# A mixer stage whose decay exponentials take their bias on ScalarE, whose GpSimd products and weight parts move to VectorE, and whose pooled and gate pieces take turns

## The chip, the cores and the metric

One core of a Trainium2 chip runs the whole program in a single launch. The metric is the device time of one execution in microseconds (us). The engines are named as in the profile: PE is TensorE (PEld its weight loads), DVE is VectorE, ACT is ScalarE, POOL is GpSimd, SP is SyncE, whose queue issues most of the loads.

## What is computed

Two transformer blocks in float32 for one sequence of 512 tokens and width 1024. The change touches only the first stage, the hybrid mixer of the first block:

```
proj = u @ w_in
z, xbc, dt_raw, v = split(proj)                        # gate, conv input, step size, pooled path
xbc = silu(causal_depthwise_conv(xbc, conv_w, conv_b))
xs, bm, cm = split(xbc)                                # 16 heads of 64; 2 groups of B and C
dt = softplus(dt_raw + dt_bias);  adt = dt * -exp(a_log)
a_cs = cumsum(adt)  in chunks of 128
seg = exp(where(causal, a_cs[l] - a_cs[s], -inf))      # decay, per head and chunk
y_diag = (C B^T * seg) @ (xs * dt)                     # within a chunk
y_off  = C @ carried_state * exp(a_cs)                 # from the chunks before
y = rmsnorm((y_diag + y_off + d_skip * xs) * silu(z))
y_pool = (window means of v, minus v) @ pool_w * pool_scale
h = x + concat(y, y_pool) @ w_out_mix
```

Cross attention, two gated MLPs, a stick-breaking attention and a sparse attention follow, and are the same before and after.

## The kernel before

Activations lie with features on the 128 partitions and the 512 tokens along the row. Float32 products of full accuracy are made of three matmuls: every operand is split into a high part in a reduced format and the low rest. A weight **piece** is 128 output features by 1024 inputs (1024 columns of float32, 512 KB); `Weights` fetches pieces on SP's queue in the order of the list that `_plan` writes, ScalarE makes the high part `wh` (L340), and `lo` makes the low part `wl` as a subtraction (L349): on VectorE, or on GpSimd for the seven pieces named in `POOL_LO` (L29): xs3, xs5, C1, v1, v4, v6 and v7. A piece is then 24 matmuls of 512 columns in `group` (all recorded at the helper's line L538). Parts are made up to two pieces ahead.

The order of all work is that of the Python text (the scheduler is manual); each engine takes its own instructions in that order. The mixer's function `_mix` (L709) runs:

- lead: B0, C0 and dt, while the input is split; then xs0.
- nine pieces xs1, xs2, xs3, B1, C1, xs4 to xs7 (L749). After each, `conv` (L880) runs a convolution on its result in three steps over three pieces: scaling and the first tap (L900, L903), three taps on VectorE (L906) and a tanh on ScalarE, and the final product (L914).
- in the background, one step after each piece: `g_dt` (L943), the step size. It ends in `adt` (L987), from which eight small matmuls form cumulated sums, and the matrix `stk` of split sums (L1006). A chain of a log series runs there, two operations per coefficient on GpSimd (L974 to L978), in a step of its own.
- `g_pair` (L1011), once for each of the eight xs pieces (two heads each), in three steps, none before `g_dt` has ended: step one transposes xs, makes `xc` and `xd` (L1025), spreads the cumulated sums over a bank by matmuls from `stk`, subtracts the column of sums `acs` on VectorE (L1035) and takes the exponential on ScalarE (L1038); step two makes the chunk states from `xd`, multiplies the decay `d` by the scores `cb` on GpSimd (L1052), and carries the states on (L1059); step three multiplies `d` by `xc` and the states by C on TensorE, and adds up (L1072 to L1074, the last on GpSimd).
- eight pooled pieces v0 to v7 (L758), each with 1 to 4 window additions on VectorE (`pool_v`, L1076), and behind every second of them the products with `pool_w` (`pool_mm`); then eight gate pieces z0 to z7 (L770), each with a tanh and two products (`g_z`, L785: L789 on VectorE, L791 on GpSimd, L793 on VectorE) and the sum of squares.

Banks of PSUM are taken from a pool of eight and go back when their readers are done.

Of the kernel before, what the change touches and what calls it, by code (L numbers as in the profile page):

```python
# [14 lines left out]
ALU = mybir.AluOpType  # L15
# [3 lines left out]
P = 128  # L19
# [9 lines left out]
POOL_LO = {"xs3", "xs5", "C1", "v1", "v4", "v6", "v7"}  # L29
# [3 lines left out]
NP = 8  # L33
FF_BLOCKS = ((0, 8), (8, 16), (16, 22))
# [13 lines left out]
def _plan(x, phases):  # L48
# [25 lines left out]
    if "mix" in phases:  # L74
# [14 lines left out]
        for j in range(8):  # L89
            add(f"v{j}", _bform(w, v0 + P * j, v0 + P * j + P))  # L90
            if j in (2, 4, 6):
                pw((j - 2) // 2)
        for j in range(8):
            add(f"z{j}", _bform(w, P * j, P * j + P))
            if j == 0:
                pw(3)
# [369 lines left out]
class Kernel:  # L466
# [242 lines left out]
    def _mix(self):  # L709
# [48 lines left out]
        for j in range(8):  # L758
            ps = self.bank()
            self.group(ps, self.W.get(f"v{j}"), xh, xl, range(KT), True, True)  # L760
            self.W.ahead()
            if j < 2:
                self.conv()
            dd[j] = self.pool_v(j, ps)
            self.W.lo()
            self.stage()
            if j in (2, 4, 6):
                self.pool_mm((j - 2) // 2, dd, self.yp)
        n2 = self.n2 = Norm(self, EPS_A, "ssd")
        for j in range(8):  # L770
            ps = self.bank()
            self.group(ps, self.W.get(f"z{j}"), xh, xl, range(KT), True, True)
            while any(p[2] <= j for p in self.pairs):
                self.stage(2)
            self.W.ahead()
            g = self.g_z(j, ps)
            next(g)
            self.W.lo()
            self.stage(3)
            self.bg.append(g)  # L780
            if j == 0:
                self.pool_mm(3, dd, self.yp)
        self.drain()

    def g_z(self, j, ps):  # L785

        nc, y = self.nc, self.y[:, j, :]
        t, th = self.tmp("t", bufs=3), self.tmp("pv", (P, 528), bufs=3)[:, :T]
        nc.vector.scalar_tensor_tensor(t, ps, 0.5, self.R, op0=ALU.mult, op1=ALU.mult)  # L789
        nc.scalar.activation(th, t, AF.Tanh)  # L790
        nc.gpsimd.tensor_tensor(t, t, y, op=ALU.mult)  # L791
        yield
        nc.vector.scalar_tensor_tensor(y, th, 1.0, t, op0=ALU.add, op1=ALU.mult)  # L793
        self.n2.tile(y)
# [128 lines left out]
    def g_cb(self, g):  # L923
# [14 lines left out]
        nc.vector.tensor_copy(cb, ps)  # L938
        nc.vector.tensor_copy(bt, pt[:, :384])
# [3 lines left out]
    def g_dt(self, ps, rtm):  # L943
# [29 lines left out]
        gp = nc.gpsimd  # L973
        gp.tensor_tensor(z2, z, z, op=ALU.mult)  # L974
        gp.tensor_scalar(q, z2, 1.0 / 17, 0.0, op0=ALU.mult, op1=ALU.add)
        for n in (15, 13, 11, 9, 7, 5, 3):
            gp.tensor_scalar(q, q, 1.0, 1.0 / n, op0=ALU.mult, op1=ALU.add)
            gp.tensor_tensor(q, q, z2, op=ALU.mult)  # L978
        yield
# [17 lines left out]
        acs, last = t64("acs"), t64("last")  # L997
        nc.vector.tensor_copy(acs, pa[:, 0:64].rearrange("p (c h) -> p c h", c=4))
        dec = t64("dec")
        tt(last, pa[:, 64:128].rearrange("p (c h) -> p c h", c=4), acs, ALU.subtract)  # L1000
# [8 lines left out]
        self.dt, self.acs, self.dec, self.cd = dt, acs, dec, cd  # L1009

    def g_pair(self, k):  # L1011
# [17 lines left out]
        for j in range(2):  # L1029
# [21 lines left out]
        for j in range(2):  # L1051
            nc.gpsimd.tensor_tensor(dm[j], dm[j], self.cbT[g], op=ALU.mult)  # L1052
# [1164 lines left out]
```

## Time and profile before

| | |
|---|---|
| runs of the kernel | 2213.94, 2212.48, 2205.34 us (median 2212.48) |
| the profiled execution | 2205.24 us, span 2203.5 us, mean granted clock 0.993 |
| PE busy | 2130.0 us, 97% of the span |
| PEld, DVE, ACT, POOL busy | 1730.3, 1231.0, 876.1, 261.2 us |
| the mixer stage | about the first 250 us of the span |

Matmuls are pipelined, so PE's busy time is not PE at its peak. A row of the windows view gives a stretch, its length, the busy time of each engine with the number of its instructions, PEclk (the share of full clock that was granted: 1.00 is 2.4 GHz, 0.50 is 1.2 GHz), the share of the DMA engines and GB/s. A row of the waits view names who waited for whom, the sum in us, how often, and the longest. A row of the groups view gives line, engine, operation, output and inputs, sizes and count, then the busy time in us and the mean of one in ns, then the idle time before them and what ended it. A row of the timeline gives start, duration, engine, line, operation and count; operations of an engine overlap a little at their ends, so the distance from one start to the next is what an operation costs in a queue.

### The profile page before, as it was taken

To read this page: it belongs to the slowest core of one execution; us is meant where nothing else is said; L and a number is where in the kernel's file an instruction comes from. 1 tells how busy PE (TensorE), PEld (TensorE's weight loads), DVE (VectorE), ACT (ScalarE), POOL (GpSimd) and SP (SyncE) were. 2 spreads that over 40 slices of the span, in tenths; PEclk is the share of its full clock that TensorE was granted. 3 is DMA by queue.
4 is the path that set the end of the run, shared out by engine and by line. 5 is a ranking of instruction groups with operands and counts; after the bars stand their busy time and mean duration, and the time that the engine had idled before them with its cause. 6 is when DMAs were issued, how large, how long until landed. Compare 5 with 4: busy or idle time off the path is not lost.

```text
span 2203.5 us, 26617 instructions
## 1 busy us (share of the span) xinstructions
PE 2130.0 (97%) x10250; PEld 1730.3 (79%) x10250; DVE 1231.0 (56%) x2032; ACT 876.1 (40%) x1405; POOL 261.2 (12%) x324
## 2 busy tenths in 40 slices
PE   8899999999999999999999999999988899999998
PEld 6687888888888888777688888888766668888886
DVE  6988756554443435567655343446668755534334
ACT  4424434343222224355534232334547644423322
POOL 1333100000000000122200000001037730000000
PEclk9999999999999999999999999999999999999999
DMA  4222444123333323322143333334431123333331
GB/s 147 63 72 77 134 122 152 57 72 96 97 97 101 98 84 108 124 77 67 48 124 97 104 95 97 96 96 127 129 98 26 26 60 103 109 101 97 96 97 66
DMA packets 63375, 205.93 MB, mean 93 GB/s; under 512 B 7952, under 2 KB 8336, under 8 KB 63120
## 3 DMA queue, kind: packets, MB, share of 16 engines
q1 hardware_dynamic: 59504, 196.86, 30.1%
q10 hardware_dynamic: 3744, 7.37, 1.0%
q8 instruction: 80, 1.31, 0.2%
q14 instruction: 47, 0.39, 0.1%
HBM read 189.39 MB, written 6.29 MB: 89 GB/s over the span
## 4 chain that ended last, share of the span: by engine, by line
PE 78%; DVE 10%; ACT 4%; POOL 4%; issue 3%; DMA 1%; SPq 0%; ACTq 0%; POOLq 0%; DVEq 0%
PE psum L538 62%; PE b L538 14%; POOL sph L1683 1%; DVE wl L349 1%; ACT sT L1665 1%; ACT sT L1666 1%; DVE t L906 1%; PE psum L2090 1%; DVE spl L1688 1%; DVE sT L1660 1%; DVE np L2068 1%; DMA nq<-nq 1%; DVE pv L1087 0%; DVE sT L1659 0%; POOL np L2082 0%
## 5 line engine op out<-in xcount | busy, mean ns | idle before, releaser
L538 PE MATMUL psum<-xh,wh 128*128 128x512 f32 x1560 | 609.9, 391 | 1.5 <-DVE h L626 0.9
L538 PE MATMUL psum<-xh,wl 128*128 128x512 f32 x1560 | 607.5, 389 | 1.6 <-DVE wl L349 1.5
L538 PE MATMUL psum<-xl,wh 128*128 128x512 f32 x1560 | 607.2, 389 | 0.0
L340 ACT ACTIVATE wh<-ws 128x1024 fp32r<-128x1024 f32 (+1 forms) x346 | 356.5, 1039 | 371.7 <-PE psum L538 315.0
L349 DVE TENSOR_TENSOR wl<-ws,wh 128x1024 fp32r<-128x1024 f32 (+2 forms) x339 | 411.4, 1219 | 98.6 <-ACT wh L340 98.4
L538 PEld LDWEIGHTS psum<-xh,wl 128*128 128x128 f32 x1560 | 292.3, 187 | 64.8 <-DVE wl L349 2.9
L538 PEld LDWEIGHTS psum<-xh,wh 128*128 128x128 f32 x1560 | 292.4, 187 | 63.2 <-issue 2.3
L538 PEld LDWEIGHTS psum<-xl,wh 128*128 128x128 f32 x1560 | 292.4, 187 | 60.5
L538 PE MATMUL b<-xh,wh 128*128 128x512 f32 (+1 forms) x488 | 194.4, 398 | 6.6 <-ACT wh L340 6.6
L538 PE MATMUL b<-xh,wl 128*128 128x512 f32 (+1 forms) x488 | 191.9, 393 | 2.2 <-POOL wl L349 1.9
L538 PE MATMUL b<-xl,wh 128*128 128x512 f32 (+1 forms) x488 | 191.6, 393 | 0.0
L538 PE MATMUL psum<-hh,wh 128*128 128x512 f32 x320 | 125.0, 391 | 0.0
L538 PE MATMUL psum<-hh,wl 128*128 128x512 f32 x320 | 124.5, 389 | 0.0
L538 PE MATMUL psum<-hl,wh 128*128 128x512 f32 x320 | 124.5, 389 | 0.0
L1354 DVE TENSOR_TENSOR h<-h,psum 128x512 f32<-128x512 f32 x48 | 33.1, 689 | 161.2 <-PE psum L538 161.2
L1345 ACT ACTIVATE t<-t 128x512 f32<-128x512 f32 x64 | 40.5, 633 | 187.9 <-DVE t L1344 187.9
L538 PEld LDWEIGHTS b<-xh,wh 128*128 128x128 f32 (+1 forms) x488 | 92.0, 188 | 26.3 <-ACT wh L340 7.0
L538 PEld LDWEIGHTS b<-xh,wl 128*128 128x128 f32 (+1 forms) x488 | 91.5, 188 | 24.6 <-POOL wl L349 2.4
L538 PEld LDWEIGHTS b<-xl,wh 128*128 128x128 f32 (+1 forms) x488 | 92.1, 189 | 19.8 <-DVE xl L551 0.8
L1344 DVE SCALAR_TENSOR_TENSOR t<-psum,r_mlp 128x512 f32<-128x512 f32 x64 | 44.2, 690 | 79.1 <-PE psum L538 79.0
L538 PE MATMUL psum<-ks,nq 128*128 128x256 f32 (+2 forms) x256 | 72.6, 376 | 16.3 <-DVE nmx L2068 9.4
L2082 POOL TENSOR_SCALAR np<-np,nsm,gates 128x512 f32<-128x512 f32 (+3 forms) x128 | 81.8, 644 | 39.2 <-PE psum L2090 20.5
(488 smaller groups left out, 2947.1 us busy)
## 6 DMA issues: line engine op xcount, KB each, us to landing
ws<-in_wst SPq DMA_DIRECT2D x332, 512.0 KB, 3.5
h<-in_xT SPq DMA_DIRECT2D x16, 256.0 KB, 3.6
kk<-kk SPq DMA_DIRECT2D x16, 256.0 KB, 3.6
nq<-nq SPq DMA_DIRECT2D x16, 256.0 KB, 2.9
ws<-in_wst SPq DMA_DIRECT2D x8, 384.0 KB, 3.1
spill<-back SPq DMA_DIRECT2D x8, 256.0 KB, 2.0
back<-spill ACTq DMA_DIRECT2D x8, 256.0 KB, 3.6
spill<-h ACTq DMA_DIRECT2D x8, 256.0 KB, 5.7
```

The costliest lines, as they stand in the source:

```text
L340: self.nc.scalar.activation(hi[:, :n], s, AF.Copy)
L349: e.tensor_tensor(lo[:, :n], s, hi[:, :n].bitcast(F32), op=ALU.subtract)
L538: self.nc.tensor.matmul(ps, a, b, start=start, stop=stop, skip_group_check=again)
L906: nc.vector.scalar_tensor_tensor(t, u[:, q:q + T], cw[:, q:q + 1], t, op0=ALU.mult, op1=ALU.add)
L1344: nc.vector.scalar_tensor_tensor(t, ps, 0.0, norm.bc, op0=ALU.max, op1=ALU.mult)
L1345: nc.scalar.activation(t, t, AF.Square)
L1354: nc.vector.tensor_tensor(self.h[:, m, :], self.h[:, m, :], ps, op=ALU.add)
L1660: self.nc.vector.tensor_scalar(tb, zb[:, :, :384], 30.0, None, op0=ALU.min)
L1665: self.nc.scalar.activation(t, t, AF.Exp)
L1666: self.nc.scalar.activation(t, t, AF.Ln, bias=1.0)
L1683: self.nc.gpsimd.tensor_scalar(hi, t, 1.0, 0.0, op0=ALU.mult, op1=ALU.add)
L2082: self.nc.gpsimd.tensor_scalar(u["p"], u["p"], u.pop("sm"), self.gates[:, u["c"], e:e + 1], op0=ALU.mult, op1=ALU.mult)
```

## The change

Five edits, all in the mixer:

1. `POOL_LO` is empty: the seven weight splits on GpSimd go to VectorE.
2. The step-size chain is on VectorE, in one step: one operation per coefficient where there were two, and no pause between them and what follows. Since the step goes, `adt` and all behind it come one piece earlier in the program.
3. The decay's difference is no operation of its own any more: VectorE makes the negative column of sums `nacs` in place of `acs`, and ScalarE adds it as the bias of the exponential, which runs on four 128-column parts, one per chunk, straight from the matmuls' bank.
4. The product of decay and scores and the gate's product go from GpSimd to VectorE; the copies of `cb` and `btm` out of PSUM go from VectorE to ScalarE.
5. The pooled and gate pieces, and the products with `pool_w`, come in one mixed order, `VZ`; the weight list follows it. The second half of a gate piece runs behind the next piece's matmuls.

```diff
-POOL_LO = {"xs3", "xs5", "C1", "v1", "v4", "v6", "v7"}
+POOL_LO = set()
...
+VZ = (("v", 0, None), ("v", 1, None), ("v", 2, 0), ("z", 0, None), ("v", 3, None), ("z", 1, None),
+      ("v", 4, 1), ("z", 2, None), ("v", 5, None), ("z", 3, None), ("v", 6, 2), ("z", 4, None),
+      ("v", 7, None), ("z", 5, None), ("z", 6, 3), ("z", 7, None))
...
-        for j in range(8):
+        n2 = self.n2 = Norm(self, EPS_A, "ssd")
+        gz = iter(())
+        for kind, j, g in VZ:
             ps = self.bank()
...
+            self.group(ps, self.W.get(f"{kind}{j}"), xh, xl, range(KT), True, True)
+            next(gz, None)
+            if kind == "v":
+                self.W.ahead()
+                if j < 2:
+                    self.conv()
+                dd[j] = self.pool_v(j, ps)
+                self.W.lo()
+                self.stage()
+            else:
+                while any(p[2] <= j for p in self.pairs):
+                    self.stage(2)
+                self.W.ahead()
+                gz = self.g_z(j, ps)
+                next(gz)
+                self.W.lo()
+                self.stage(3)
+            if g is not None:
+                self.pool_mm(g, dd, self.yp)
+        next(gz, None)
         self.drain()
...
-        nc.gpsimd.tensor_tensor(t, t, y, op=ALU.mult)
+        nc.vector.tensor_tensor(t, t, y, op=ALU.mult)
...
-        nc.vector.tensor_copy(cb, ps)
-        nc.vector.tensor_copy(bt, pt[:, :384])
+        nc.scalar.activation(cb, ps, AF.Copy)
+        nc.scalar.activation(bt, pt[:, :384], AF.Copy)
...
-        gp = nc.gpsimd
-        gp.tensor_tensor(z2, z, z, op=ALU.mult)
-        gp.tensor_scalar(q, z2, 1.0 / 17, 0.0, op0=ALU.mult, op1=ALU.add)
+        tt(z2, z, z, ALU.mult)
+        nc.vector.tensor_scalar(q, z2, 1.0 / 17, None, op0=ALU.mult)
         for n in (15, 13, 11, 9, 7, 5, 3):
-            gp.tensor_scalar(q, q, 1.0, 1.0 / n, op0=ALU.mult, op1=ALU.add)
-            gp.tensor_tensor(q, q, z2, op=ALU.mult)
-        yield
+            nc.vector.scalar_tensor_tensor(q, q, 1.0 / n, z2, op0=ALU.add, op1=ALU.mult)
...
-            nc.vector.tensor_tensor(
-                d.rearrange("p (c l) -> p c l", c=4), pa.rearrange("p (c l) -> p c l", c=4),
-                self.acs[:, :, h:h + 1].to_broadcast([P, 4, P]), op=ALU.subtract)
-            nc.scalar.activation(d, d, AF.Exp)
+            for c in range(4):
+                s = slice(P * c, P * c + P)
+                nc.scalar.activation(d[:, s], pa[:, s], AF.Exp, bias=self.nacs[:, c, h:h + 1])
...
-            nc.gpsimd.tensor_tensor(dm[j], dm[j], self.cbT[g], op=ALU.mult)
+            nc.vector.tensor_tensor(dm[j], dm[j], self.cbT[g], op=ALU.mult)
```

How the order moves, at three places. First VectorE's queue at the step-size chain, from the reciprocal to `adt`. Before (`t_441` is the convolution of xs2, `wl_492` the split of xs4; the series on `dtq` is on GpSimd, between the product on `dtz` and L980):

```order
L971 RECIPROCAL dtz<-dtz 128x64
L953 TENSOR_TENSOR dtz<-dtz,dte 128x64
L906 SCALAR_TENSOR_TENSOR t_441<-pv_438,cw,t_441 128x512 x3
L899 MEMSET pv_498 128x3
L900 TENSOR_TENSOR pv_498<-b_466,r_in 128x512
L349 TENSOR_TENSOR wl_492<-ws_348,wh_491 128x1024
L914 SCALAR_TENSOR_TENSOR h<-h,t_384 128x512
L980 SCALAR_TENSOR_TENSOR dtq<-dtq,dtz 128x64
L981 TENSOR_SCALAR dtx<-dtx 128x64
L953 TENSOR_TENSOR dtv<-dtq,dtx 128x64
L983 TENSOR_SCALAR dtv<-dtv 128x64
L987 SCALAR_TENSOR_TENSOR adt<-dtv,a_exp 128x64
```

The same stretch of VectorE's queue in the changed kernel:

```order
L971 RECIPROCAL dtz<-dtz 128x64
L953 TENSOR_TENSOR dtz<-dtz,dte 128x64
L953 TENSOR_TENSOR dtz_399<-dtz 128x64
L974 TENSOR_SCALAR dtq<-dtz_399 128x64
L976 SCALAR_TENSOR_TENSOR dtq<-dtq,dtz_399 128x64 x7
L977 SCALAR_TENSOR_TENSOR dtq<-dtq,dtz 128x64
L978 TENSOR_SCALAR dtx<-dtx 128x64
L953 TENSOR_TENSOR dtv<-dtq,dtx 128x64
L980 TENSOR_SCALAR dtv<-dtv 128x64
L984 SCALAR_TENSOR_TENSOR adt<-dtv,a_exp 128x64
L906 SCALAR_TENSOR_TENSOR t_441<-pv_438,cw,t_441 128x512 x3
```

The three taps, the scaling, the split and the final product that stood inside the chain now stand behind it.

Second, TensorE's queue where it needs `adt`. Before (`wl_432` is the low part of piece C1, `wh_491` the high part of xs4, `small` holds the triangle of ones):

```order
L538 MATMUL b_569<-xh_97,wl_432 128x512
L538 MATMUL b_611<-adt,small 128x64
L538 MATMUL b_611<-adt,ones 128x64
L538 MATMUL b_612<-small,adt 16x128 x4
L538 MATMUL b_630<-xh_97,wh_491 128x512
```

TensorE's queue in the changed kernel (`wl_375` is the low part of piece B1, `wh_431` the high part of C1):

```order
L539 MATMUL b_517<-xh_97,wl_375 128x512
L539 MATMUL b_558<-adt,small 128x64
L539 MATMUL b_558<-adt,ones 128x64
L539 MATMUL b_559<-small,adt 16x128 x4
L539 MATMUL b_581<-xh_97,wh_431 128x512
```

The matmuls from `adt` stand behind B1 now, one piece of 24 matmuls earlier; the first pair's matmuls from `stk` follow one piece later in both kernels, then behind C1 instead of xs4.

Third, VectorE's queue at the second step of the first pair. Before (`ct` is the convolution of C1, `xc_756` and `xd_757` belong to the second pair, as `d_763` and `d_769` do):

```order
L349 TENSOR_TENSOR wl_724<-ws_562,wh_723 128x1024
L914 SCALAR_TENSOR_TENSOR ct_661<-ct_661,t_605 128x512
L1059 SCALAR_TENSOR_TENSOR prev_745<-prev_745,cd,b_739 128x64 x4
L1025 TENSOR_TENSOR xc_756<-b_751,dtv 128x512
L1025 TENSOR_TENSOR xd_757<-b_751,dec 128x384
L1035 TENSOR_TENSOR d_763<-b_760,acs 128x512
L1035 TENSOR_TENSOR d_769<-b_766,acs 128x512
```

The same step in the changed kernel (`d_635` and `d_643` are the first pair's decays, `cb_577` the scores):

```order
L350 TENSOR_TENSOR wl_679<-ws_505,wh_678 128x1024
L914 SCALAR_TENSOR_TENSOR bt_612<-bt_612,t_552 128x512
L1049 TENSOR_TENSOR d_635<-d_635,cb_577 128x512
L1049 TENSOR_TENSOR d_643<-d_643,cb_577 128x512
L1056 SCALAR_TENSOR_TENSOR prev_701<-prev_701,cd,b_695 128x64 x4
L1023 TENSOR_TENSOR xc_712<-b_707,dtv 128x512
L1023 TENSOR_TENSOR xd_713<-b_707,dec 128x384
```

Two differences per pair have left VectorE's queue and two products have come in, a step later in the pair.

## Rows read from the trace of the kernel before

**Rows 1.** Windows of 40 us in the mixer (columns: as described above).

```profile
80.00:120.00 40.00, 36.06 (x199) 29.19 (x197) 38.98 (x58) 16.71 (x28) 15.76 (x12) 0.96 0.20 59
160.00:200.00 40.00, 38.07 (x192) 30.78 (x191) 36.27 (x57) 14.75 (x24) 10.70 (x9) 1.00 0.31 91
```

**Rows 2.** Waits of TensorE in the first 330 us (sum, times, longest).

```profile
PE b L538 <- POOL d L1052: 5.8, 5, 1.8
PE b L538 <- DVE adt L987: 4.3, 1, 4.3
PE b L538 <- POOL wl L349: 1.9, 1, 1.9
PE b L538 <- DVE xd L1025: 1.9, 1, 1.9
PE b L538 <- DVE stk L1006: 1.1, 1, 1.1
```

**Rows 3.** Windows of 2 us at the ends of the low clock's stretches.

```profile
68.00:70.00 2.00, 0.00 (x0) 0.00 (x0) 1.93 (x4) 0.00 (x0) 1.47 (x1) 0.60 0.00 0
...
74.00:76.00 2.00, 2.00 (x8) 1.59 (x7) 1.97 (x4) 1.18 (x2) 0.00 (x0) 0.69 0.00 0
...
108.00:110.00 2.00, 1.43 (x15) 1.10 (x16) 2.00 (x4) 0.86 (x2) 0.52 (x1) 0.84 0.00 0
...
112.00:114.00 2.00, 2.00 (x10) 1.32 (x9) 2.00 (x5) 0.00 (x0) 1.20 (x2) 0.81 0.76 240
...
214.00:216.00 2.00, 1.58 (x15) 1.25 (x16) 0.58 (x2) 2.00 (x4) 0.37 (x1) 0.79 0.03 8
...
218.00:220.00 2.00, 2.00 (x10) 1.74 (x10) 1.30 (x2) 1.18 (x3) 0.24 (x1) 0.85 0.88 264
```

**Rows 4.** Groups of instructions by shape in the first 270 us.

```profile
L906 DVE SCALAR_TENSOR_TENSOR t<-pv,cw,t 128x512 f32<-128x512 f32 x36 | 36.5, 1015 | 3.1 <-ACT t L903 2.2
L349 DVE TENSOR_TENSOR wl<-ws,wh 128x1024 fp32r<-128x1024 f32 x27 | 33.3, 1235 | 11.3 <-ACT wh L340 11.2
...
L793 DVE SCALAR_TENSOR_TENSOR h<-pv,t 128x512 f32<-128x512 f32 x8 | 13.1, 1642 | 0.0
...
L1035 DVE TENSOR_TENSOR d<-b,acs 128x512 f32<-128x512 f32 x16 | 10.2, 680 | 0.0
L1038 ACT ACTIVATE d<-d 128x512 f32<-128x512 f32 x16 | 9.8, 633 | 23.5 <-DVE d L1035 23.5
L903 ACT ACTIVATE t<-pv,cbias,cw 128x512 f32<-128x512 f32 x12 | 9.8, 817 | 4.7 <-DVE pv L900 4.3
...
L1074 POOL TENSOR_TENSOR h<-h,ex 128x384 f32<-128x384 f32 x8 | 8.1, 1009 | 49.5 <-DVE ex L1073 36.3 <-DVE pv L1081 13.2
...
L1054 ACT ACTIVATE prev<-b 128x128 f32<-128x128 f32 x8 | 2.1, 259 | 0.0
```

**Rows 5.** Timeline of VectorE and GpSimd, from xs3's split to the first pair.

```profile
44.99 4.29 DVE L906 SCALAR_TENSOR_TENSOR t<-pv,cw,t 128x512 f32<-128x512 f32 x3 [0.37 <-ACT t L903]
45.99 2.75 POOL L349 TENSOR_TENSOR wl<-ws,wh 128x1024 fp32r<-128x1024 f32 x1 [26.61 <-ACT wh L340]
...
57.65 0.18 DVE L970 TENSOR_SCALAR dtz<-dte 128x64 f32<-128x64 f32 x1
...
70.25 0.23 DVE L987 SCALAR_TENSOR_TENSOR adt<-dtv,a_exp 128x64 f32<-128x64 f32 x1
...
81.57 2.33 DVE L906 SCALAR_TENSOR_TENSOR t<-pv,cw,t 128x512 f32<-128x512 f32 x3
...
88.43 4.13 DVE L906 SCALAR_TENSOR_TENSOR t<-pv,cw,t 128x512 f32<-128x512 f32 x3
```

**Rows 6.** The chain that ended last: one piece of 24 matmuls on TensorE.

```profile
28.37 5.59 PE b L538 x24
```

**Rows 7.** Timeline of TensorE: the first and the second pair's matmuls from `xd`.

```profile
88.26 0.83 PE L538 MATMUL b<-xd,btm 128*128 128x128 f32 x6
...
97.82 0.83 PE L538 MATMUL b<-xd,btm 128*128 128x128 f32 x6
```

More of the change, by code (lines that the diff above doesn't have):

```diff
@@ L88, in _plan @@
                 add(f"xs{j}", _bform(w, xs0 + P * j, xs0 + P * j + P))
-        for j in range(8):
[L90 to L96, printed above, removed]
+        for kind, j, g in VZ:
+            c = (v0 if kind == "v" else 0) + P * j
+            add(f"{kind}{j}", _bform(w, c, c + P))
+            if g is not None:
+                pw(g)
         for m in range(8):
@@ L757, in _mix @@
         dd = {}
-        for j in range(8):
+        n2 = self.n2 = Norm(self, EPS_A, "ssd")
+        gz = iter(())
+        for kind, j, g in VZ:
             ps = self.bank()
[L760 to L782, printed above, removed]
+            self.group(ps, self.W.get(f"{kind}{j}"), xh, xl, range(KT), True, True)
[15 more added lines that the diff above has]
+                self.stage(3)
+            if g is not None:
+                self.pool_mm(g, dd, self.yp)
+        next(gz, None)
         self.drain()
@@ L996, in g_dt @@
             self.mm(pr[:16, P * c:P * c + P], adt[:, c, :], upper, True, True)
-        acs, last = t64("acs"), t64("last")
-        nc.vector.tensor_copy(acs, pa[:, 0:64].rearrange("p (c h) -> p c h", c=4))
+        nacs, last = t64("nacs"), t64("last")
+        nc.vector.tensor_scalar(nacs, pa[:, 0:64].rearrange("p (c h) -> p c h", c=4), -1.0, None,
+                                op0=ALU.mult)
         dec = t64("dec")
-        tt(last, pa[:, 64:128].rearrange("p (c h) -> p c h", c=4), acs, ALU.subtract)
+        tt(last, pa[:, 64:128].rearrange("p (c h) -> p c h", c=4), nacs, ALU.add)
         nc.scalar.activation(last, last, AF.Exp)
@@ L1008, in g_dt @@
         yield
-        self.dt, self.acs, self.dec, self.cd = dt, acs, dec, cd
+        self.dt, self.nacs, self.dec, self.cd = dt, nacs, dec, cd
     def g_pair(self, k):
```

## The prediction

> **What bounds the kernel now.** I read the page first (the table above): TensorE is the one engine that is busy nearly all the time. So the kernel is a long line of matmuls, and an edit off TensorE can only win back time in which TensorE waits, or runs at the lower of its two clocks. The change touches the mixer stage alone, roughly the stretch from 40 to 245 us. There the windows show VectorE nearly full: 39.0 of 40 us busy from 80 to 120, 36.3 of 40 from 160 to 200 [rows 1]. An engine that full, with an in-order queue, is late with whatever stands at its end. The list of TensorE's waits says what it is late for: GpSimd's products of decay and scores (5.8 us in five waits), `adt` at the end of the step-size chain (4.3 in one), a weight split on GpSimd (1.9), `xd` (1.9), the row `stk` (1.1) [rows 2]. They sum to 15.0.
>
> The second cost is the clock. The granted clock drops from 2.4 GHz (1.00) to 1.2 GHz (0.50) after three of these waits [rows 3]. A window of 2 us at 0.60 holds 1.6 us at the low level, so the first low stretch begins at 68.4 and, by the 0.69 of the window from 74, ends at 75.2; TensorE works in it from 70.5, so half of 4.7 us is lost, 2.4. The second goes from 109.4 to 112.8 and the third from 215.2 to 218.6; each is 3.4 long and loses 1.7. The single 1.9 us wait for `xd` lies inside the window from 160 to 200, whose clock is 1.00 throughout [rows 1]: a lone wait of that length did not bring the clock down, one of 4.3 did, and so did, twice, two shorter ones close together from the line of GpSimd's products, the longest of which is 1.8. So TensorE loses 15.0 + 2.4 + 1.7 + 1.7 = **20.8 us** in this stage, and that is the most that the change can return. It issues the same number of instructions before and after.
>
> **Why VectorE is late: GpSimd holds it up.** A trio of convolution taps takes 2.33 us in an undisturbed place, and 4.29 where it meets GpSimd's split that started at 45.99 and took 2.75 [rows 5]. By groups the tap averages 1.015 us where an undisturbed one takes a third of 2.33, 0.78, 36 times: 8.6 us. The gate's last product (L793) averages 1.642 where the tap, as large, takes 0.78: 8 times 0.86 is 6.9 [rows 4]. So at least 15 us of VectorE's busy time are waiting. What the rows show is that an operation that meets GpSimd takes the other's whole rest on top of its own time. The Trainium skill says so too (SBUF — State Buffer, section "SBUF: two separate sides"): the two engines share a port pair, whoever starts first holds it for the whole instruction, and the other is blocked rather than slowed. By that rule, the trace agrees with its 2.33 and 4.29, the stretch goes wholly where GpSimd's work goes, and stays at the eight final adds (L1074), which the change leaves on GpSimd.
>
> **VectorE's ledger.** Out: 16 differences (L1035) at 0.680 are 10.9, and the copies of cb and btm (two of each, priced as one operation of 512 and one of three quarters of it) some 2.4: 13.3. In: 7 splits at 1.235 are 8.6 [rows 4]; 16 products with cb and 8 gate products, which no row shows on VectorE; each is half a split, 0.62, to a difference, 0.68. I take 0.65, near either: 15.6. And 9 small operations of the chain at `adt`'s 0.23 [rows 5], say 0.25 from start to start: 2.3. In all 26.5 in, 13.3 out, at least 15.5 of stretch gone: 2 us less than now. That is a bound from the safe side, since other groups are stretched as well.
>
> **ScalarE.** 16 exponentials of 512 columns become 64 of 128 with a bias column. A plain one of 128 columns takes 0.259 [rows 4]; the convolution's first tap, 512 columns with scale and bias from columns, takes 0.817 against the exponential's 0.633, so two columns cost 0.18 and one perhaps 0.09. 64 at 0.26 to 0.35 are 17 to 22 us, where 16 at 0.633 were 10, and the four copies add 2.4. ScalarE works 16.7 of 40 us from 80 to 120 [rows 1], and VectorE's turn before the exponential falls away, so I cost this at nothing. With that cover gone it would be 1 us a pair.
>
> **Walking the path.** (a) The split of xs3 starts on VectorE when GpSimd's did, at 45.99, and is through after 1.2, at 47.2, not at 48.7: **0.5 us** remain of 1.9.
> (b) The chain. VectorE reaches its first operation at 57.65 [rows 5]. Ahead of it now stand two splits (2.4) and 1.0 of waiting for the first one's input; two stretched trios give back 2 times 1.96. So it comes there 0.5 earlier, at 57.2. Then sixteen operations lead to the end of `adt`; the diff turns two GpSimd operations per coefficient into one. At 0.25 and a little more for the reciprocal that is 4.3 (ends: 0.23 each, 3.7, and 0.33 each, 5.3): `adt` is there at 61.5 instead of 70.5. But its matmuls stand one piece earlier in TensorE's queue, as the order rows show. TensorE came to them at 70.5 - 4.3 = 66.2; it now comes one piece (5.6 [rows 6]) and 1.4 of saved waiting earlier, at 59.2. **2.3 us** of waiting remain: less than half the expected prize, since the chain and the place that needs it both moved.
> (c) `stk`. From `adt` to the first operation behind `stk` VectorE took 81.57 - 70.25 = 11.3 [rows 5]. The copies of cb and btm leave it (1.2), a split enters (1.2). So `stk` is there at 61.3 + 11.3 = 72.6. Before, TensorE's wait of 1.1 ended at 81.6, so it came there at 80.5, 9.9 after `adt` at 70.5 [rows 2, 5], 2.4 of it lost to the low clock; one piece stands between them before and after. It gets there between 69.1 and 71.4 and waits **3.5 or 1.2 us**, against 1.1 before. If the clock falls at (b), its 2.4 and the 1.2 make 3.6; if it does not, 3.5 of waiting, and then a fall behind it costs another 1.7. VectorE sets this moment either way. So (c) costs 3.5 to 5.2, I take 4.4.
> (d) From there, piece by piece with one pair in each. TensorE takes 97.82 - 88.26 = 9.56 from one pair's `xd` matmuls to the next one's [rows 7]. VectorE took 88.43 - 81.57 = 6.86 for taps, split, `xc`, `xd` and two differences [rows 5], undisturbed; the two products now stand for the differences, and the step's other operations come on top: four of 64 columns for the carried states at `adt`'s 0.23, and the skip and offset products at a difference's 0.68 and three quarters of it, 2.1 in all, an estimate: 9.0. VectorE gains 0.6 a piece on TensorE, which no longer waits here. Of the five waits for GpSimd's products those in this stretch go, and the second low stretch with its 1.7.
> (e) The pooled and gate pieces in turn. A pooled piece gives VectorE up to four window additions, a gate piece none, so the pairs' products no longer queue behind two heavy pieces in a row. The wait for `xd`, the rest of the five and the third low stretch go, but the products follow the window additions in the queue and may be late by nothing to their own 1.3. I take **0.5**. The loads on SyncE's queue keep their number and move with the pieces; GpSimd's splits no longer hold them back.
>
> **The sum.** Left afterwards: 0.5 + 2.3 + 4.4 + 0.5 = 7.7 of 20.8. The gain is **13.1 us** (by the ends above 11 to 15). The profiled execution took 2205.24 and would take 2192.1. It is 7.2 under the median of the runs, 2212.48, whose three values lie at 2205 and at 2213 to 2214; I give the forecast against the median: **2199.4**.
>
> **Rivals.** *VectorE stays just too slow (0.27).* The final adds (1.009 [rows 4]) still hold it for about 1 us a pair, and the longer exponentials may hold it another 0.9. 9.0 becomes 10.9 against 9.56, TensorE waits 1.3 in four to eight pairs, with one more fall of the clock: 5 to 10 plus 1.7 given back, the gain is 1 to 6: about 2209. For it: the margin of 0.6 is thin, and (c) starts with VectorE late. Against: in the undisturbed stretches VectorE kept up. What the Trainium skill says of the held port (the page and section above) bears on this rival alone: by it the final adds block.
> *Slower: VectorE becomes the bound and the clock goes with it (0.06).* If the stretch were VectorE's own, its 13.2 net of new work would lie on the path; with a wait in every pair the clock would stay at 1.2 GHz over much of 73 to 113, where TensorE works 36 us, and cost up to 18. -20.8 + 13.2 + 18 is +10.4: 2223. It decides when VectorE needs some 1.5 us more than 9.56 per piece and pair. Against: trios with no GpSimd work beside them take 2.33.
> *More comes back (0.12).* The chain is quicker and `stk` early enough to keep the clock up: 3 us stay lost, the gain is 18, 2194.5.
> The forecast has 0.55.
>
> **How the numbers follow.** A measurement of this kernel can tell about 0.5% from no change, 11 us here: below 2201.4 or above 2223.5. The forecast's ends are 2197.5 to 2201.5, and the median of a few runs can fall to either of the two levels that the runs show, so some of the 0.55 falls under "same". With the third rival and nine tenths of the forecast: 0.60 faster, 0.36 the same, 0.04 slower. The range reaches from the third rival's side with half the runs' spread below the forecast, 2189, to the first rival's 2209 and most of the same above it, 2212.
>
> **What would show it.** `adt` near 61 and TensorE's wait for it near 2.3; the wait for `stk` longer than 1.1; no waits for GpSimd; trios of 2.3 throughout save beside final adds; clock 1.00 from 80 to 245. If VectorE's `d` or `prev` shows up in TensorE's waits with over 5 us in sum, the first rival holds. If trios still take over 4 us with GpSimd idle, my reading of the stretch is wrong.

## The result and the profile after

The changed kernel takes **2190.7 us** (median of 4 runs, 2190.05 to 2191.70); the kernel before took 2210.9 beside it (4 runs, 2205.34 to 2213.94). The ratio is 0.9913 with a 95% interval of 0.9899 to 0.9928: faster by 16 to 22 us, more than the forecast's 13.1 and inside its range of 2189 to 2212. The profiled executions stand at 2205.24 and 2190.76, 14.5 apart, their spans at 2203.5 and 2187.8.

The mixer stage is measured by itself with two small groups of matmuls: from the start of the one that sums the input norm (`acc_in`) to the start of the one that sums the gate's norm (`acc_ssd`). The timeline of TensorE gives for the changed kernel (start, duration, engine, line, operation):

```profile
28.01 0.95 PE L402 MATMUL b<-ones,acc_in 128*128 128x1 f32 x8
255.12 0.95 PE L402 MATMUL b<-ones,acc_ssd 128*128 128x1 f32 x8
```

That is 227.1 us. The same two rows of the kernel before start at 27.43 and 270.26: 242.8; the stage ends at 270 there, not at the "about 250" of the table above. So **the stage gives back 15.7**, as much as the spans differ; the executions differ by 1.2 less, and that lies outside the spans. The edits moved many lines, by up to three; L906 is still the taps.

TensorE's waits in the first 330 us, which answer to [rows 2] (the 6.6 for `wh` and one of 0.3 for `wl` end before 12 us; the kernel before has them too, with 6.6 and 0.2):

```profile
PE b L539 <- ACT wh L341: 6.6, 1, 6.6
PE b L539 <- DVE adt L984: 2.2, 1, 2.2
PE b L539 <- DVE stk L1004: 1.9, 1, 1.9
PE b L539 <- DVE wl L350: 0.7, 2, 0.4
```

GpSimd is gone from the list, and so is `xd`. The windows of 40 us, as in [rows 1], and those of 2 us in which the clock was low, as in [rows 3]:

```profile
80.00:120.00 40.00, 40.00 (x240) 32.65 (x239) 38.29 (x71) 20.76 (x48) 5.55 (x6) 1.00 0.19 60
160.00:200.00 40.00, 39.91 (x212) 32.35 (x212) 35.20 (x65) 17.30 (x38) 2.75 (x3) 1.00 0.20 61
```

```profile
62.00:64.00 2.00, 1.95 (x12) 1.48 (x12) 1.93 (x3) 0.00 (x0) 0.00 (x0) 0.70 0.00 0
64.00:66.00 2.00, 2.00 (x6) 1.40 (x5) 2.00 (x5) 1.70 (x3) 0.00 (x0) 0.50 0.00 0
66.00:68.00 2.00, 2.00 (x9) 1.59 (x9) 1.97 (x3) 0.70 (x1) 0.00 (x0) 0.94 0.47 104
```

VectorE is as full as before from 80 to 120 (38.3 of 40 us against 39.0), yet TensorE no longer waits there. The clock is low once, for 3.4 us (1.2 of the first window, all of the second, 0.2 of the third), against three stretches before, and from 68 on it stays at 1.00. Groups by shape in the first 260 us, against [rows 4], and the chain and `stk` in VectorE's timeline, against [rows 5]:

```profile
L906 DVE SCALAR_TENSOR_TENSOR t<-pv,cw,t 128x512 f32<-128x512 f32 x36 | 27.0, 750 | 2.7 <-ACT t L903 1.8
L1035 ACT ACTIVATE d<-b,nacs 128x128 f32<-128x128 f32 x64 | 17.3, 381 | 2.9 <-PE b L539 2.9
L1049 DVE TENSOR_TENSOR d<-d,cb 128x512 f32<-128x512 f32 x16 | 11.1, 735 | 0.0
L1071 POOL TENSOR_TENSOR h<-h,ex 128x384 f32<-128x384 f32 x8 | 9.9, 1236 | 103.0 <-DVE ex L1070 103.0
L791 DVE TENSOR_TENSOR t<-t,h 128x512 f32<-128x512 f32 x8 | 5.5, 692 | 5.9 <-ACT pv L790 5.9
L793 DVE SCALAR_TENSOR_TENSOR h<-pv,t 128x512 f32<-128x512 f32 x8 | 5.5, 681 | 0.0
```

```profile
57.47 0.19 DVE L970 TENSOR_SCALAR dtz<-dte 128x64 f32<-128x64 f32 x1
...
61.77 0.23 DVE L984 SCALAR_TENSOR_TENSOR adt<-dtv,a_exp 128x64 f32<-128x64 f32 x1
...
72.45 0.68 DVE L1004 TENSOR_TENSOR stk<-b,stk 16x512 fp32r<-16x512 f32 x1 [0.35 <-ACT stk L1003]
```

### The profile page after: what moved, and what is told of

The parts are those of the page before. It is cut to its first block, busy times and chain, and to the rows that moved or that the text cites. A ratio compares the mean times of both kernels' runs of the same rounds, so it can differ in the third digit from the quotient of the medians.

```text
span 2187.8 us, 26618 instructions
## 1 busy us (share of the span) xinstructions
PE 2126.4 (97%) x10250; PEld 1728.4 (79%) x10250; DVE 1218.1 (56%) x2052; ACT 885.0 (40%) x1457; POOL 203.2 (9%) x277
## 4 chain that ended last, share of the span: by engine, by line
PE 83%; DVE 7%; ACT 4%; POOL 3%; issue 2%; DMA 1%; ACTq 0%; POOLq 0%; SPq 0%; DVEq 0%
PE psum L539 63%; PE b L539 18%; POOL sph L1680 1%; ACT sT L1662 1%; ACT sT L1663 1%; PE psum L2087 1%; DVE spl L1685 1%; DVE wl L350 1%; DVE np L2065 1%; DVE sT L1657 1%; DMA nq<-nq 1%; DVE t L906 0%; DVE sT L1656 0%; POOL np L2079 0%; DVE st L1608 0%
## 5 line engine op out<-in xcount | busy, mean ns | idle before, releaser
L350 DVE TENSOR_TENSOR wl<-ws,wh 128x1024 fp32r<-128x1024 f32 (+1 forms) x346 | 417.2, 1212 | 97.9 <-ACT wh L341 97.8
L539 PE MATMUL psum<-ks,nq 128*128 128x256 f32 (+2 forms) x256 | 72.5, 376 | 16.4 <-DVE nmx L2065 9.5
```

The costliest lines, as they stand in the source:

```text
L350: e.tensor_tensor(lo[:, :n], s, hi[:, :n].bitcast(F32), op=ALU.subtract)
L539: self.nc.tensor.matmul(ps, a, b, start=start, stop=stop, skip_group_check=again)
```

## The experiments

The question was which part carried the 15.7. The prediction had named GpSimd's hold on VectorE as the reason why VectorE was late. The table has all kernels; "stage" is `acc_in` to `acc_ssd`, "waits" is the sum of TensorE's waits from 30 to 290 us, and "low" the time at 1.2 GHz in the stage, from windows of 2 us. The last three columns are of the one profiled execution. It lies within 2 us of the kernel's median, save for the kernel before (5.7 below), run 5 (3.6 below) and run 7 (7.9 above). The expectations name the time at which the stage ends (270.3 before, 255.1 changed), the table its length. The kernel before had a median of 2208.9 to 2209.8 in these sessions.

| | median (runs, range) | ratio to before, 95% | stage | waits | low |
|---|---|---|---|---|---|
| before | 2210.9 (4, 2205.3 to 2213.9) | | 242.8 | 15.0 | 13.7 |
| changed | 2190.7 (4, 2190.1 to 2191.7) | 0.9899 to 0.9928 | 227.1 | 4.5 | 3.4 |
| 1 products back | 2191.4 (5, 2191.0 to 2197.2) | 0.9909 to 0.9934 | 229.3 | 6.1 | 6.8 |
| 2 differences back | 2195.8 (5, 2195.0 to 2199.1) | 0.9927 to 0.9952 | 231.7 | 6.9 | 6.8 |
| 3 idle GpSimd work | 2198.9 (5, 2193.0 to 2199.9) | 0.9929 to 0.9954 | 231.6 | 7.7 | 6.8 |
| 4 chain later | 2194.5 (5, 2193.4 to 2195.7) | 0.9917 to 0.9944 | 227.8 | 5.0 | 3.4 |
| 5 order back | 2194.2 (6, 2190.6 to 2199.1) | 0.9923 to 0.9956 | 228.9 | 4.9 | 6.8 |
| 6 order alone | 2203.8 (11, 2202.2 to 2206.0) | 0.9974 to 0.9992 | 239.5 | 13.0 | 10.3 |
| 7 GpSimd freed alone | 2205.5 (12, 2202.8 to 2213.4) | 0.9978 to 1.0002 | 243.7 | 14.5 | 13.7 |
| 8 early splits | 2189.9 (5, 2189.5 to 2192.2) | 0.9906 to 0.9938 | 225.6 | 4.4 | 0 |
| 9 differences alone | 2196.7 (5, 2194.8 to 2198.5) | 0.9924 to 0.9954 | 233.6 | 8.9 | 6.8 |
| 10 chain back | 2192.6 (5, 2192.3 to 2197.6) | 0.9911 to 0.9939 | 229.7 | 5.9 | 6.9 |
| 11 steps first | 2188.9 (4, 2186.6 to 2189.7) | 0.9887 to 0.9915 | 226.8 | 3.7 | 3.4 |
| 12 steps first, pair later | 2184.9 (5, 2184.6 to 2188.3) | 0.9876 to 0.9908 | 221.6 | 1.4 | 0 |

### One part undone: runs 1, 2, 5 and 10

**Run 1, products back on GpSimd.**

```diff
-            nc.vector.tensor_tensor(dm[j], dm[j], self.cbT[g], op=ALU.mult)
+            nc.gpsimd.tensor_tensor(dm[j], dm[j], self.cbT[g], op=ALU.mult)
...
-        nc.vector.tensor_tensor(t, t, y, op=ALU.mult)
+        nc.gpsimd.tensor_tensor(t, t, y, op=ALU.mult)
```

> The changed kernel with one part undone: the 16 products with cb and the 8 gate products run on GpSimd again. Theory (GpSimd's operations hold VectorE up, and TensorE waits for what VectorE then brings late): the taps' mean of 0.750 us rises towards 0.85 or more, the gate's last product from 0.681 to over 1.2, TensorE again waits for GpSimd's d by 3 to 6 us and the clock falls once or twice in the pairs (1.7 each); 5 to 9 us slower than the changed kernel. Rival A (what counted is the order of the pieces, which now leaves each product a whole piece of 9.6 us): the waits for d stay away, within 2 us of the changed kernel.

The waits of TensorE from 40 to 290 us, and two of the groups:

```profile
PE b L539 <- DVE stk L1004: 3.5, 1, 3.5
PE b L539 <- DVE adt L984: 2.2, 1, 2.2
PE b L539 <- DVE wl L350: 0.4, 1, 0.4
```

```profile
L906 DVE SCALAR_TENSOR_TENSOR t<-pv,cw,t 128x512 f32<-128x512 f32 x36 | 31.3, 869 | 2.7 <-ACT t L903 1.8
L1049 POOL TENSOR_TENSOR d<-d,cb 128x512 f32<-128x512 f32 x16 | 25.4, 1609 | 2.2 <-ACT d L1035 2.1
```

The products take 1.6 us each and stretch the taps from 0.750 to 0.869, as the theory said, and no wait for `d` comes of it: rival A held. The stage is 2.2 longer for another reason. Up to the first pair this kernel issues the same instructions as the changed one, but the clock did not fall after the wait for `adt`. TensorE therefore came to `stk` sooner, waited 3.5 instead of 1.9, and the clock fell there, for 6.8 us:

```profile
68.00:70.00 2.00, 1.02 (x7) 0.65 (x5) 2.00 (x5) 1.45 (x2) 0.00 (x0) 1.00 0.02 8
70.00:72.00 2.00, 0.00 (x0) 0.00 (x0) 1.29 (x5) 1.19 (x4) 0.00 (x0) 0.78 0.58 156
72.00:74.00 2.00, 1.50 (x4) 0.70 (x5) 1.90 (x4) 1.44 (x3) 0.00 (x0) 0.50 0.26 107
...
76.00:78.00 2.00, 2.00 (x6) 1.63 (x5) 2.00 (x4) 2.00 (x9) 0.65 (x1) 0.51 0.32 57
```

TensorE works from 72.5 to 78 at half the clock and loses 2.75. With the two waits that is 8.45, against 2.2 + 1.9 + 1.7 = 5.8 in the changed kernel: 2.65 of difference, more than the 2.2 of the stage. Where the products run costs no wait here.

**Run 2, differences back on VectorE.**

```diff
-            for c in range(4):
-                s = slice(P * c, P * c + P)
-                nc.scalar.activation(d[:, s], pa[:, s], AF.Exp, bias=self.nacs[:, c, h:h + 1])
+            nc.vector.tensor_tensor(
+                d.rearrange("p (c l) -> p c l", c=4), pa.rearrange("p (c l) -> p c l", c=4),
+                self.nacs[:, :, h:h + 1].to_broadcast([P, 4, P]), op=ALU.add)
+            nc.scalar.activation(d, d, AF.Exp)
```

> The changed kernel with one part undone: VectorE again makes the 16 decay differences (0.68 each, now by adding the negated sums) and ScalarE's exponentials are 16 of 512 columns. VectorE's load per piece and pair rises by 1.36, from the 9.0 of the prediction to 10.4, against TensorE's 9.56. Theory: TensorE waits 0.8 for most of the first pairs, 3 to 6 us in all, plus one fall of the clock (1.7): 4 to 8 slower than the changed kernel. Rival B (the 9.0 was too high; VectorE has slack enough in every piece once GpSimd is quiet): within 1 us of the changed kernel.

The theory held in kind: 5.1 slower, with three new waits for `d`, 2.4 in sum where it said 3 to 6. With one more low stretch (1.7) that is 4.1 of the stage's 4.6. But this low stretch begins at 72.6, behind the wait of 1.9 for `stk` that the changed kernel has as well, and ahead of VectorE's first difference:

```profile
72.00:74.00 2.00, 1.86 (x6) 1.17 (x7) 1.90 (x3) 1.08 (x2) 0.00 (x0) 0.66 0.09 37
```

```profile
77.68 1.28 DVE L1033 TENSOR_TENSOR d<-b,nacs 128x512 f32<-128x512 f32 x2
```

So the differences are shown to cost the 2.4 of waits, and the fall is not shown to be theirs. This also measures ScalarE's side: 64 exponentials of 128 columns with a bias, 0.381 each, cost TensorE no wait in the changed kernel.

**Run 5, order back**: `VZ` replaced by v0 to v7, then z0 to z7, with the products by `pool_w` behind v2, v4, v6 and z0.

> The changed kernel with one part undone: all pooled pieces first and then all gate pieces, as before. The first run of this study (products back on GpSimd) cost 1.4 us of the mixer stage, the second (differences back on VectorE) 3.4, together far from the 15 that the change returned there. Theory (the order carries the rest, because pooled pieces with a pair each overload VectorE): TensorE waits for xd or d among the later pooled pieces by 3 to 6 us and the clock falls once or twice; the stage ends 5 to 9 us later than the changed kernel's 255.1. Rival D (each part alone is enough, since GpSimd is quiet and the differences are gone): no new wait, the stage ends within 1 us of 255.1.

Neither. One wait of 1.8 for `d` is new, against 3 to 6 expected; against it stands a wait for `stk` of 0.4 instead of 1.9. The rest is a low stretch of 6.8 us behind `adt` where the changed kernel has 3.4, in a place where both issue the same instructions. This profile lies 3.6 under the median of run 5, so other executions may lose more.

**Run 10, chain back on GpSimd.**

```diff
-        tt(z2, z, z, ALU.mult)
-        nc.vector.tensor_scalar(q, z2, 1.0 / 17, None, op0=ALU.mult)
+        gp = nc.gpsimd
+        gp.tensor_tensor(z2, z, z, op=ALU.mult)
+        gp.tensor_scalar(q, z2, 1.0 / 17, 0.0, op0=ALU.mult, op1=ALU.add)
         for n in (15, 13, 11, 9, 7, 5, 3):
-            nc.vector.scalar_tensor_tensor(q, q, 1.0 / n, z2, op0=ALU.add, op1=ALU.mult)
+            gp.tensor_scalar(q, q, 1.0, 1.0 / n, op0=ALU.mult, op1=ALU.add)
+            gp.tensor_tensor(q, q, z2, op=ALU.mult)
+        yield
```

> The changed kernel with one part undone: 16 operations of the step-size polynomial run on GpSimd, one piece lies between them and the rest, and the matmuls on adt stand one piece later in TensorE's queue, as before. Theory (the prediction's step b: with GpSimd idle otherwise, the old chain ends at about 67 to 69, and TensorE comes to it at 65.4): the wait for adt is 1.5 to 3.5 with the clock falling behind it; VectorE saves 2.3 us of small operations but waits for GpSimd in their place; the stage ends at 254.5 to 258 (255.1 with the chain on VectorE). Rival (the chain in one go is worth what it took off before, 2.1 of waiting and 0.7 of clock): a wait of 4 us or more, the stage ends at 258 or later.

As the theory said: the wait for `adt` is 3.0 where it was 2.2, that for `stk` 1.9 in both, one of 0.6 for `d` is new, and the clock falls twice. The second fall stands behind the wait of 1.9 for `stk`, which the changed kernel has too without one, so only the 0.8 and the 0.6 are shown to be the chain's.

Undone singly, then, the parts bring 0, 2.4, 1.8 and 1.4 us of new waits for products, differences, order and chain, leaving out the wait for `stk`, which grew or shrank with the clock ahead of it. Neither the splits nor the copies of `cb` and `btm` were undone by themselves.

### One part alone: runs 6, 7 and 9

**Run 6** is the kernel before with `VZ` and its loop alone.

> The kernel before with one part of the change alone: pooled and gate pieces in turn. The waits for adt (4.3), wl (1.9) and stk and the low clock from 68.4 to 75.2 (2.4) stay, for they stand ahead of it. Theory (order carries most of what the pairs lose): of the 11.1 us that the pairs lose before (5.8 for d, 1.9 for xd, 1.7 and 1.7 of low clock) 7 to 11 go, and the stage ends at 259 to 263 instead of 270.3. Rival E (GpSimd's holds, which stay, are what makes d late): waits for GpSimd's d of 4 us or more remain, with at least one fall of the clock; the stage ends at 266 or later.

**Run 7** is the kernel before with `POOL_LO = set()` and the two products of run 1 on VectorE.

> The kernel before with one part of the change alone: the seven splits and the 24 products leave GpSimd for VectorE (the step-size polynomial, the differences and the order of the pieces stay). Theory (held VectorE is worth about what the operations cost it, and the pieces' order and the differences still overload it): the wait for wl shortens by 1.5, the pairs' waits change their name from GpSimd's d to VectorE's d and xd and stay 4 to 8 us in sum; the stage ends at 264 to 269 instead of 270.3. Rival F (the prediction's reading: GpSimd's hold is the loss): no waits for d, taps of 0.78 throughout, the stage ends at 258 to 261.

**Run 9** is the kernel before with `nacs`, the biased exponentials, and ScalarE's copies of `cb` and `btm`.

> The kernel before with one part of the change alone: the differences become ScalarE's bias column, and cb and btm are copied on ScalarE; GpSimd keeps its splits, products and polynomial. The losses ahead of the pairs stay (wl 1.9, adt 4.3, low clock 2.4, stk about 1). Theory G (VectorE's own load in the pairs decides, whoever holds it: 13.3 us leave it): of the 11.1 us that the pairs lose before, 7 to 10 go, and the stage ends at 260 to 263 instead of 270.3. Rival E (GpSimd is late with the products, and holds VectorE): waits for GpSimd's d of 3 us or more and at least one fall of the clock stay; the stage ends at 266 or later.

The waits of TensorE from 30 to 290 us in run 7, and its taps:

```profile
PE b L538 <- DVE d L1052: 6.4, 5, 2.9
PE b L538 <- DVE adt L987: 2.9, 1, 2.9
PE b L538 <- DVE stk L1006: 2.9, 1, 2.9
PE b L538 <- DVE h L1072: 1.9, 1, 1.9
PE b L538 <- DVE wl L349: 0.4, 1, 0.4
```

```profile
L906 DVE SCALAR_TENSOR_TENSOR t<-pv,cw,t 128x512 f32<-128x512 f32 x36 | 27.0, 750 | 2.7 <-ACT t L903 1.8
```

The same in run 9:

```profile
PE b L538 <- DVE adt L987: 4.3, 1, 4.3
PE b L538 <- POOL wl L349: 1.9, 1, 1.9
PE b L538 <- POOL d L1052: 1.4, 3, 0.8
PE b L538 <- DVE pv L1081: 1.1, 1, 1.1
PE b L538 <- DVE stk L1007: 0.2, 1, 0.2
```

```profile
L906 DVE SCALAR_TENSOR_TENSOR t<-pv,cw,t 128x512 f32<-128x512 f32 x36 | 37.1, 1032 | 3.4 <-ACT t L903 2.5
```

These two decide. Run 7 has the taps at an undisturbed 0.750 and loses as much as before: 14.5 of waits against 15.0, 13.7 us of low clock in both. (By the medians it is 3.4 faster, with an interval from 5 faster to no change; its profiled execution lies 7.9 above its median, that of the kernel before 5.7 below.) Five waits for GpSimd's `d` became five for VectorE's. Rival F, which was the prediction's reading, is out, and the theory, which gave it 1 to 6 us, still gave too much. Run 9 leaves the taps stretched to 1.032 and gains 9.3 of the stage's 15.7: the pairs' waits fall from 5.8 + 1.9 to 1.4 + 1.1, and the losses ahead of the pairs (`wl`, `adt`, 6.8 us of low clock behind it) are all that stays. Theory G held. Run 6 gained 3.3: it lost the wait for `xd` and one low stretch, and kept six waits for `d`, which is rival E:

```profile
PE b L539 <- POOL d L1052: 6.0, 6, 1.6
```

So **the differences are the part that counts**: with the copies of `cb` and `btm` they alone give 9 of 15.7, the order alone 3, GpSimd freed alone nothing in the stage. By the medians the three are 12.6, 5.0 and 3.4 of 20. What the runs do not separate is the share of the copies, and why a difference weighs so much: it is 0.68 of VectorE's time, but it also stands between TensorE's matmul and ScalarE's exponential, in a full queue, and both go at once.

**Run 3** adds work on GpSimd to the changed kernel, at the place of the products; nothing reads it.

```diff
             nc.vector.tensor_tensor(dm[j], dm[j], self.cbT[g], op=ALU.mult)
+            for s in (slice(0, 256), slice(256, T)):
+                nc.gpsimd.tensor_tensor(self.tmp("junk", (P, 256), bufs=1), self.cbT[g][:, s],
+                                        self.R[:, s], op=ALU.mult)
```

> The changed kernel with 32 added GpSimd multiplications of 256 columns, four per pair at the place of the products; nothing reads what they write. Theory (held VectorE): each takes 0.6 to 0.8 us of GpSimd and holds VectorE for most of it, so VectorE's groups in the pairs' stretch lengthen by 10 to 20 us in sum and TensorE waits 3 to 10 us more. Rival A or B (only GpSimd's own lateness with the products counted, or VectorE has slack enough): no wait of TensorE that was not there, within 1 us of the changed kernel.

It brings GpSimd's hold out by itself. The operations were longer than expected, 1.032 each, 33.0 in sum. The taps rise to 0.810, and three waits for `d`, 1.5 in sum, are new; the other 3 of the stage's 4.5 are the same longer wait for `stk` with its fall of the clock as in run 1, ahead of the first added operation. So the hold is real, and 33 us of work on GpSimd cost TensorE 1.5 by it.

### Where the last waits come from: runs 4, 8, 11 and 12

Run 4 puts one `yield` ahead of the matmuls on `adt` and one ahead of the end of `g_dt`.

> The changed kernel with the matmuls on adt one piece later in TensorE's queue, and the first pair one piece later again. Theory (the waits for adt and stk are the chain's place alone): both waits, 2.2 and 1.9, and the low clock behind the first, 1.7, go and nothing comes in their place: 4 to 6 us faster than the changed kernel. Rival C (VectorE is behind by a fixed amount of work there, and eight pairs in two pieces less leave it too little room): 2 us or more of new waits in the pairs or at their end, gain under 3 us, or a loss.

Rival C: both waits went, 4.1 in sum, and 3.6 for `xd` and 1.0 for `d` came. That fits a VectorE that is behind by a fixed amount of work when the pairs begin. Run 8 takes run 4 and moves two splits into VectorE's idle time ahead of the first convolution:

```diff
         norm.ssq()
+        self.W.make(self.W.i + 2)
...
         self.conv("B0", lead[0][1])
+        self.W.make(self.W.i + 3)
```

> The changed kernel with the step-size chain's matmuls and the first pair one piece later each, as in the fourth run, and with the splits of two weight pieces (2 times 1.22 on VectorE, 1.04 each on ScalarE) moved ahead of the first convolution, where VectorE stands idle for 4.1 us (31.4 to 35.5) and twice for 0.9. Theory C (VectorE enters the pairs with a fixed debt of work; a wait removed at one place comes back at the next): the debt falls by 2.4 us, of the fourth run's waits for xd (3.6) and d (1.0) about 2.2 stay and the clock stays up, so the stage ends at 251 to 252.5 instead of 255.1 and the kernel is 3 to 4 us faster than the changed one, if the later stages fall as there. Rival (the idle time ahead is needed by something there, such as the first convolution): new waits before 60, no gain.

The stage is 1.5 shorter than the changed kernel's, 2.2 shorter than run 4's, against a debt made smaller by 2.4. Most of the gain is in the clock, which did not fall, though TensorE waited 3.0 us for `xd`. The waits fell from 5.0 to 4.4 only, where theory C said by 2.4, and the median is 0.8 below the changed kernel's, where it said 3 to 4: the size of the debt is not confirmed by this run. Run 11 has run 8's early splits without its `yield`s; it makes `xd` ahead of `xc` and lets the chain and the pairs' steps pass the convolutions:

```diff
             self.W.ahead()
-            self.conv(nme, ps)
             self.stage(2)
+            self.conv(nme, ps)
```

> The changed kernel with the two early splits of the eighth run, and in the pieces xs1 to xs7 the step-size chain and the pair's step ahead of the piece's convolution in every queue (one line moved), and xd made before xc. Theory C (the debt of VectorE can be left with the convolutions, whose results are wanted pieces later): adt is there at about 57.5 and stk at 64 to 65, TensorE waits for neither, the clock stays up, and the stage ends at 248.5 to 250.5; the kernel takes 2184 to 2187. Rival (a late convolution holds the bank that TensorE's next group needs, or the split that stands behind it): new waits for pv, for PSUM or for wl of 2 to 6 us, no gain.

A miss: `adt` was there at 56.1, but waits for `pv` (1.6), `wl` (1.1), `stk` (0.5) and `d` (0.5) and a fall of the clock stood in the place of those that went, as the rival said. A late scaling (`pv`) holds the bank that TensorE wants next. Run 12 repairs that: `for g in (q[-1], q[-2])` in `conv` puts a piece's scaling ahead of the taps of the piece before, and one `yield` puts the first pair a piece later.

> The eleventh run's kernel (early splits, steps ahead of the convolutions, xd ahead of xc) with two more edits: the first pair one piece later, and each piece's scaling pv, which frees TensorE's bank, ahead of the taps of the piece before. In the eleventh run the stage ended at 255.1, as in the changed kernel: its waits for adt (2.2) was gone, but waits for pv (1.6) and stk (0.5) and one fall of the clock (1.7) stood in its place. Theory C (the debt is about 4 us of VectorE's work, to be put where nothing waits): the waits for stk and pv go, the clock stays up, the stage ends at 251 to 252.5, at or below the eighth run's 252.8, and the kernel takes 2186 to 2189. Rival (the debt cannot be put anywhere in these pieces): 2 us or more of waits under other names and a fall of the clock, the stage ends at 254 or later.

The one wait of TensorE that is left from 30 to 290 us:

```profile
PE b L539 <- DVE d L1052: 1.4, 1, 1.4
```

The clock stays at 1.00 from 56 to 256. The stage takes 221.6, 5.5 less than in the changed kernel, and ends at 249.1, sooner than the 251 to 252.5 that theory C gave; the kernel takes **2184.9**, 1 less than it gave. That is below the changed kernel as well: its five runs (2184.6 to 2188.3) lie below all four of the changed kernel (2190.1 to 2191.7), though the intervals of the two ratios, taken in different sessions, overlap.

## Why the prediction was right, and where it was wrong

**Right: the walk along the path.** Its terms against the profile after:

| step | predicted | measured |
|---|---|---|
| (a) split of xs3 | 0.5 | 0.4 |
| (b) chain starts, `adt` there | 57.2, 61.5 | 57.47, 62.0 |
| (b) wait for `adt` | 2.3 | 2.2 |
| (c) `stk` there | 72.6 | 73.1 |
| (c) wait for `stk`, with the clock's loss | 3.5 to 5.2, taken 4.4 | 1.9 + 1.7 = 3.6 |
| (d) pairs in the xs pieces | 0 | 0 |
| (e) pooled and gate pieces | 0.5 | 0 |
| sum left of 20.8 | 7.7 | 6.2 |

The gain by these terms is 14.6, and the stage shows 15.7; where the other 1.1 comes from no row tells. Two small slips are in its sums: (a)'s own rows leave 0.4, and seventeen operations, not sixteen, lead to `adt`. Step (c) was right in its mechanism: VectorE sets the moment, so what the clock loses less behind `adt` is waited more for `stk`. With the fall the two are 1.7 + 1.9, said 2.4 + 1.2; without it the wait is 3.5, as said, in runs 1 and 3, but the fall behind it then cost 2.75 in run 1, said 1.7. In (d) VectorE was to need 9.0 of TensorE's 9.56 per piece: busy 38.3 of 40 us, it needs 9.2. The items of VectorE's ledger held as well. Stretch gone: 36.5 - 27.0 for the taps and 13.1 - 5.5 for the gate's last product are 17.1, said at least 15.5. New products: 0.735 and 0.692, said 0.65. ScalarE's exponentials were longer than said (0.381 against 0.26 to 0.35), and hidden as said. TensorE, clock and waits did in the pairs what "What would show it" asked for.

**Wrong: "Why VectorE is late: GpSimd holds it up".** The hold is there: the taps' mean is 0.750 with GpSimd quiet, 0.869 with the products on it, 1.015 with the splits too. The Trainium skill's rule of the shared port pair (SBUF — State Buffer, section "SBUF: two separate sides"), by which the engine that starts first blocks the other, agrees with these means, though a mean cannot tell blocking from slowing. But ending the hold by moving the work to VectorE was not what TensorE gained by. The stage as one window shows VectorE's busy time (the third pair of columns), before, in run 7, in run 9 and after:

```profile
27.43:270.26 242.83, 227.69 (x1143) 184.57 (x1142) 203.78 (x331) 98.97 (x158) 71.88 (x62) 0.97 0.28 83
27.21:270.89 243.68, 228.87 (x1144) 184.88 (x1143) 201.24 (x362) 98.86 (x158) 19.14 (x31) 0.97 0.26 83
28.05:261.62 233.57, 224.64 (x1144) 181.97 (x1142) 193.27 (x311) 107.74 (x210) 71.24 (x62) 0.99 0.27 87
28.01:255.12 227.11, 222.56 (x1144) 180.96 (x1143) 192.24 (x352) 108.49 (x210) 14.10 (x15) 0.99 0.29 90
```

Freeing GpSimd alone leaves VectorE 2.5 us less busy, since the splits and products that come eat up the stretch that goes; taking the differences and copies out leaves it 10.5 less busy, though the taps stay stretched. The ledger gave minus 2 for all edits, called a bound, where 11.5 came: a sum that hid which edit did the work. Its own items, 15.5 of stretch against 24.2 of splits and products, and 13.3 for the differences and copies, could have told which. Runs 7 and 9 show the two apart, +0.9 and -9.3 us of stage.

**Wrong by 7 us: the offset from the profiled execution to the median.** The forecast set the gain of 13.1 against the median, 7.2 above the profiled execution. The measured median, 2190.7, lies 7 under the forecast's own ends (2197.5 to 2201.5), and inside the range only because that was drawn down to 2189 for the third rival. 2205.24 - 13.1 is 2192.1, and the profiled execution took 2190.76; so did the median of the changed kernel. The offset was no constant. Run 7 shows what it can consist of: the execution profiled there took 2213.39, others down to 2202.76, and it has low stretches of the clock, far behind the mixer, that the profiles of the kernel before and of the changed one do not have:

```profile
1732.00:1736.00 4.00, 3.55 (x12) 1.23 (x14) 1.63 (x7) 0.96 (x4) 1.86 (x3) 0.72 0.30 66
1736.00:1740.00 4.00, 4.00 (x31) 2.86 (x28) 1.22 (x8) 1.60 (x6) 0.41 (x1) 0.85 0.02 4
1772.00:1776.00 4.00, 1.93 (x10) 1.18 (x8) 3.83 (x16) 3.54 (x11) 2.48 (x5) 0.84 0.36 80
1776.00:1780.00 4.00, 4.00 (x11) 1.18 (x12) 0.78 (x3) 0.00 (x1) 1.07 (x2) 0.50 0.24 51
1780.00:1784.00 4.00, 4.00 (x30) 2.73 (x27) 1.07 (x5) 1.45 (x4) 0.26 (x1) 0.80 0.00 0
```

That the slower runs of the kernel before are of this kind is likely, but none of their profiles is on record; it stays open, and with it nearly 6 of the 20 us between the medians.

**The rivals.** VectorE stayed fast enough in the pairs, so the first did not come, nor did the slower one. The hold that the first one counted on is there, but small: two products took 2.11 us beside the final add that started at 92.42 and 1.28 with no GpSimd work beside them, and over all 16 the mean is 0.735 each. The third, 18 us, was nearest to what the medians showed, but its reasons did not come: the chain was no quicker than forecast (`adt` at 62.0), TensorE waited 1.9 for `stk`, and the clock fell once, behind `adt`. That its number came near is luck.

## What to carry to other kernels

Draw the ledger of a full engine edit by edit and not only in sum: work that moves onto it can eat all the time that the move frees. Look first for the operation that stands on the full engine between two others and can be folded into one of them; here a bias column took it away at no cost to TensorE. And when an engine is behind with its work at some point, a wait removed there can come back at the next place: move work into its idle time ahead, or let what is needed soon pass what is needed later, and watch whose buffers the postponed work holds.

## What was not expected of the hardware

The same wait does not always bring the clock down. Ahead of the first pair the changed kernel and runs 1 and 3 issue the same instructions; after 2.2 to 2.3 us of waiting for `adt` the granted clock fell to 0.50 in the first and stayed at 1.00 in the other two. After 1.9 us of waiting for `stk` it fell in runs 2 and 10 and stayed at 1.00 in the changed kernel. In run 8 it stayed at 1.00 through a wait of 3.0, in run 4 it fell behind one of 3.6. Each low stretch found in the stage was 3.4 or 6.8 us long, and with 1.7 us lost in each 3.4 that TensorE works through, this alone moved a stage by 2 to 3 us between kernels whose instructions up to there are the same (runs 1 and 3 against the changed one): differences of that size say nothing before the clock's rows have been read.
